# A two-layer decoder trunk on one core: one more hidden pair of the second feed-forward layer computed plainly, its operand combinations on VectorE alone, and other closing products among the last sums

## The chip, the core and the metric

The kernel runs on one core of a Trainium2 chip. The metric is the device time of one execution in microseconds; of several runs the median is given. TensorE does the matrix products, VectorE, ScalarE and GpSimd the elementwise work, SyncE issues the transfers. Each engine works through its own instructions in the order in which the program was built, and waits where a result of another engine is missing.

## The reference

A sequence of 1024 tokens of width 1024, with 16 meta tokens ahead, runs through two layers. Layer 0 mixes tokens by causal pooling, layer 1 by differential attention with 8 heads; after each mixer comes a SwiGLU feed-forward part with 2816 hidden units. All is float32.

```
def rms_norm(x, g):
    y = xf * lax.rsqrt(jnp.mean(xf * xf, axis=-1, keepdims=True) + RMS_EPS)
    return y * g
def swiglu(h, w_gate, w_up, w_down):
    return (jax.nn.silu(h @ w_gate) * (h @ w_up)) @ w_down
...
    for i in range(DEPTH):
        hn = rms_norm(h, mix_norm_g[i])
        if i % N_MIXERS == 0:
            h = h + pool_mixer(hn, pool_w[j], pool_scale[j])
        else:
            h = h + diff_attention(hn, attn_w_qkv[j], attn_w_o[j], ...)
        h = h + swiglu(rms_norm(h, ffn_norm_g[i]), ffn_w_gate[i], ffn_w_up[i], ffn_w_down[i])
    h = rms_norm(h, final_norm_g)
    return h[:, N_META:]
```

## The kernel before

**Precision.** A float32 product is made of three matmuls on rounded numbers (`mm3`, lines 167 to 172): each operand is kept as a rounded high half and a low half, the rest, and high x high, high x low and low x high are added up in PSUM. Whatever goes into a product must therefore be split first: ScalarE rounds it (a CAST), and VectorE or GpSimd subtracts the rounded half from it (`split`, line 1304, for the second feed-forward part; `split_w`, line 147, elsewhere).

**Tiles.** Activations lie with the features on the 128 partitions and tokens along the row. The feed-forward part of layer 1 (`layer1`, from line 1556) works in two halves of 512 tokens, `x[0]` and `x[1]` (x10 and x11 in the program's names), each of eight feature blocks. The 2816 hidden units are 22 slices of 128, taken as 11 pairs. For each pair, gate and up products come first, then silu(gate) x up (`acts1`, or the `use` functions), then the pair's share of the down product (`yd`), which VectorE adds to the residual `H` (`down_add`, line 1496).

**Two ways to a gate or up product.** `plain_up` (line 1381) multiplies a slice by a half of the tokens: 16 products of three matmuls for gate and up together. `wino` (line 1392) handles a pair of slices and both token halves as a 2 x 2 block product with seven block multiplications instead of eight (Strassen and Winograd). It needs combinations of weight blocks (`z`, on GpSimd, line 1420) and of token blocks. The latter, T1 to T4, serve all pairs and are made once by the generator `twist_gen` (line 1323): for each of four feature blocks k, t3 = b22 - b12, t1 = b12 - b11, t2 = b22 - t1, each from the high and low halves and split again. The differences of the high halves (`d`) run on VectorE, those of the low halves (`e`) on GpSimd, and the low half of the split on GpSimd. T4 overwrites a part of x[1] and is undone before the last pair, which is plain as well.

**The order.** Pair 0 is plain, pairs 1 to 9 use `wino`. The generator is advanced by hand between the steps of pair 0 (`next(tw)`, with `fill` of the down product). The final place of each instruction on its engine is decided by a scheduler that builds the program from a simulated timeline; only the very end is written out (`manual_schedule`).

**The attention entry.** Ahead of layer 1 the last sums of layer 0 run beside the first norm of layer 1 (`rstd_gen`, line 174: ScalarE squares each feature block, `sq`, and GpSimd adds them into `acc`; TensorE sums over partitions, `ms`, and spreads the result, `mr`). Beside it the first heads' weights are loaded and split: `proj_w` (line 880) takes head 0's three on VectorE and later heads' on GpSimd, in four pieces.

**The end.** The last pair's down product is made for tokens 0 to 511 (chunk 1), 512 to 767 (chunk 2) and 768 to 1023 (chunk 0). `final` (line 1530) closes each chunk with the final norm: eight closing products H x gain x r, six on VectorE in one instruction each (line 1550), two, of chunk 0 three, on GpSimd (line 1548) after ScalarE has applied the gain (line 1547).

Of the kernel before, what the change touches and what calls it, by code (L numbers as in the profile page):

```python
# [11 lines left out]
ALU = mybir.AluOpType  # L12
# [87 lines left out]
class Trunk:  # L100
# [73 lines left out]
    def rstd_gen(self, out, h, a, b, nm, lag=9, wide=False, ys=None):  # L174
# [1148 lines left out]
    def twist_gen(self, x):  # L1323
# [13 lines left out]
        def less(nm, a, b):  # L1337
            d = self.tt(f"{nm}d")
            V.tensor_tensor(d, a[0], b, op=ALU.subtract)
            V.tensor_tensor(d, d, a[1], op=ALU.add)  # L1340
            return d
# [13 lines left out]
        for k in range(4):  # L1355
            b11, b12, b21, b22 = ([part(j, i, hl, k) for hl in range(2)] for i in range(2) for j in range(2))
            t3 = diff(f"t3_{k}", b22, b12)
            self.split(t3, *pair(3, k), G)
            t1 = diff(f"t1_{k}", b12, b11)
            self.split(t1, *pair(1, k), G)  # L1360
            t2 = less(f"t2_{k}", b22, t1)
            self.split(t2, *pair(2, k), G)
            yield
        yield True
        for k in range(4):
            t4 = diff(f"t4_{k}", [part(0, 1, hl, k) for hl in range(2)], [t.bitcast(F32) for t in pair(2, k)])
            self.split(t4, *pair(4, k), G if k % 2 else V)
            yield
        yield True
        for k in range(4):  # L1370
            b12 = diff(f"b12_{k}", [part(0, 0, hl, k) for hl in range(2)], [t.bitcast(F32) for t in pair(1, k)], ALU.add)
# [158 lines left out]
    def final(self, c, ys=None):  # L1530
        nc, ap = self.nc, self.ap
        w, o = W1[c], OFF1[c]
        h = self.H[:, :, o : o + w]
        ro = {}
        for n, _ in enumerate(self.rstd_gen(ro, h, 0, w, f"fin{c}", FINLAG[c], c == 1, ys)):
# [3 lines left out]
            yield  # L1539
        r = ro[f"fin{c}"]  # L1540
        yield
        pk = (1, 4, 6) if ys else (1, 4)
        for k in range(KT):
            hk = h[:, k, :]
            if k in pk:
                if not ys:
                    nc.scalar.activation(hk, hk, AF.Copy, scale=self.gcol("fin", k))
# [3 lines left out]
            yield  # L1551
            if k in OUTS[c]:
                k0 = OUTS[c][k]
                nc.sync.dma_start(ap["out"].rearrange("(k p) n -> p k n", p=P)[:, k0 : k + 1, o : o + w], h[:, k0 : k + 1, :])

    def layer1(self, ox, ws, part):
        nc, tc, ap = self.nc, self.tc, self.ap
        NP = FT // 2
        with ExitStack() as right, ExitStack() as left:
# [30 lines left out]
            def plain(j, s):  # L1590
                if s not in gu:
                    gu[s] = self.gu_units(s, f"c{s}{j}")
                yield from self.plain_up(s, x, j * HALF, HALF, gu[s], s, a)
# [6 lines left out]
            drain(plain(1, 1))  # L1600
            next(tw)
            drain(plain(1, 0))
            next(tw)
            dg = self.down_gen(0, a)
            while not next(tw):
                fill(dg, 2)
            while not next(tw):
                fill(dg, 1)
            drain(dg)
            for p in range(1, NP - 1):  # L1610
                s = {}
                drain(self.gate_gen(p, x, s))
                if p > 1:
                    drain(self.down_gen(p - 1, a))
# [214 lines left out]
```

## Time and profile before

| | us |
|---|---|
| median of 3 runs | 2135.73 |
| lowest and highest run | 2135.21, 2138.09 |
| the profiled execution | 2137.84 |
| its span, first to last instruction | 2136.1 |
| TensorE busy in it | 2073.9 (97%) |
| VectorE busy | 1359.7 (64%) |
| ScalarE busy | 883.6 (41%) |
| GpSimd busy | 589.0 (28%) |

The span is what the profiler sees of the profiled execution; that execution's own time has 1.7 us more around it, and is 2.1 us above the median. PE is TensorE, DVE VectorE, ACT ScalarE, POOL GpSimd. In a row, L with a number is the line of the kernel, `out<-in` are tile names without their numbers, then come partitions x elements; brackets give the idle time of the engine ahead of the instruction and who ended it. The granted clock of TensorE is a share of its full 2.4 GHz. Consecutive instructions of one engine overlap a little, so that durations add up to more than the time from one start to the next.

### The profile page before, as it was taken

What the parts mean: (1) busy time and instruction counts of PE and PEld (TensorE: products, weight loads), DVE (VectorE), ACT (ScalarE), POOL (GpSimd) and SP (SyncE); (2) the same over time, 40 slices, a digit from 0 to 9 for tenths busy, and PEclk for the clock granted to TensorE, in tenths of its full rate; (3) what the DMA queues carried; (4) which work ended last, traced back from release to release, by engine and by line L of the source; (5) the groups of instructions that cost most, each with busy time, mean ns of one, the idle gap of its engine ahead of it and who ended that gap; (6) DMA issues with size and microseconds to landing.
All of it is one profiled execution on the core that took longest, in us unless ns stands there. A gap on an engine that the chain in (4) does not pass through costs nothing.

```text
span 2136.1 us, 30678 instructions
## 1 busy us (share of the span) xinstructions
PE 2073.9 (97%) x11958; PEld 1923.6 (90%) x11958; DVE 1359.7 (64%) x2363; ACT 883.6 (41%) x1860; POOL 589.0 (28%) x692
## 2 busy tenths in 40 slices
PE   7999999999999999999999999998999999999996
PEld 7999999999999999999999998876788888888886
DVE  6665555555555467776676777479666666666655
ACT  5533222333232235666666655342433333333223
POOL 4301111101111026443444333137312112222103
PEclk8999999999999999999999999998999999999998
DMA  7002111111110132121111146411111111111102
GB/s 251 22 22 70 40 50 50 50 60 40 40 60 20 50 116 89 43 63 42 60 63 43 53 134 207 153 41 40 60 40 60 60 59 40 60 60 40 60 21 79
DMA packets 52700, 139.30 MB, mean 65 GB/s; under 512 B 5618, under 2 KB 17435, under 8 KB 52555
## 3 DMA queue, kind: packets, MB, share of 16 engines
q1 hardware_dynamic: 52555, 137.34, 19.3%
q8 instruction: 94, 1.54, 0.3%
q14 instruction: 51, 0.42, 0.1%
HBM read 115.16 MB, written 17.90 MB: 62 GB/s over the span
## 4 chain that ended last, share of the span: by engine, by line
PE 86%; DVE 7%; ACT 3%; DMA 2%; issue 1%; POOL 0%; SPq 0%; DVEq 0%; ACTq 0%; POOLq 0%
PE pj L170 4%; PE pj L171 4%; PE pj L172 4%; PE y L170 3%; PE y L172 3%; PE y L171 3%; PE yd L170 3%; PE yd L171 3%; PE yd L172 3%; PE xw_g L172 3%; PE xw_g L170 3%; PE xw_g L171 3%; PE gu L171 3%; PE xw_u L172 3%; PE xw_u L170 3%; PE xw_u L171 3%
## 5 line engine op out<-in xcount | busy, mean ns | idle before, releaser
L170 PE MATMUL pj<-xh_m,w_h 128*128 128x348 f32 (+2 forms) x576 | 187.5, 326 | 1.3 <-DVE oo L1091 1.1
L172 PE MATMUL pj<-xh_m,w_l 128*128 128x348 f32 (+2 forms) x576 | 184.8, 321 | 0.0
L171 PE MATMUL pj<-xl_m,w_h 128*128 128x348 f32 (+2 forms) x576 | 184.3, 321 | 0.0
L1496 DVE TENSOR_TENSOR H<-H,yd 128x512 f32<-128x512 f32 (+1 forms) x184 | 120.4, 662 | 88.7 <-PE yd L172 87.5
L820 DVE TENSOR_TENSOR h<-h,y 128x348 f32<-128x348 f32 (+1 forms) x216 | 108.4, 514 | 81.7 <-PE y L172 81.6
L170 PE MATMUL yd<-ah,d 128*128 128x512 f32 (+1 forms) x368 | 141.8, 390 | 12.0 <-DVE H L1496 7.2
L1305 ACT CAST w_u<-raw_u 128x512 fp32r<-128x512 f32 x91 | 55.0, 621 | 228.5 <-PE y L172 115.3
L171 PE MATMUL yd<-al,d 128*128 128x512 f32 (+1 forms) x368 | 141.9, 386 | 0.5 <-DVE al L1306 0.5
L172 PE MATMUL yd<-ah,d 128*128 128x512 f32 (+1 forms) x368 | 140.5, 385 | 0.0
L170 PE MATMUL y<-ah,d 128*128 128x348 f32 (+1 forms) x432 | 138.3, 320 | 0.0
L171 PE MATMUL y<-al,d 128*128 128x348 f32 (+1 forms) x432 | 138.0, 320 | 0.0
L172 PE MATMUL y<-ah,d 128*128 128x348 f32 (+1 forms) x432 | 135.7, 320 | 0.0
L1306 DVE TENSOR_TENSOR w_g<-raw_g,w_g 128x512 fp32r<-128x512 f32 x91 | 76.1, 842 | 66.9 <-ACT w_g L1305 60.3
L170 PEld LDWEIGHTS pj<-xh_m,w_h 128*128 128x128 f32 x576 | 108.4, 188 | 2.2 <-DVE oo L1091 1.3
L171 PEld LDWEIGHTS pj<-xl_m,w_h 128*128 128x128 f32 x576 | 108.5, 189 | 0.7
L172 PEld LDWEIGHTS pj<-xh_m,w_l 128*128 128x128 f32 x576 | 108.3, 188 | 0.3
L1011 ACT ACTIVATE e<-s,st 128x144 f32<-128x144 f32 (+6 forms) x112 | 78.8, 705 | 39.6 <-DVE e L1021 20.0
L170 PEld LDWEIGHTS yd<-ah,d 128*128 128x128 f32 x368 | 70.6, 193 | 26.7 <-DVE H L1496 8.2
L1420 POOL TENSOR_TENSOR z<-raw_g 128x512 f32<-128x512 f32 x18 | 27.2, 1514 | 241.8 <-DVE w_u L1306 241.8
L1306 DVE TENSOR_TENSOR d<-raw_d,d 128x512 fp32r<-128x512 f32 x80 | 68.1, 863 | 39.0 <-ACT d L1305 38.9
L1305 ACT CAST w_g<-raw_g 128x512 fp32r<-128x512 f32 x91 | 56.5, 623 | 79.6 <-PE xw_u L172 35.0
L1043 DVE TENSOR_TENSOR atl<-at,ath 116x512 fp32r<-116x512 f32 (+3 forms) x112 | 62.0, 571 | 39.5 <-ACT ath L1042 39.1
(597 smaller groups left out, 6542.2 us busy)
## 6 DMA issues: line engine op xcount, KB each, us to landing
raw_d<-in_down_dram SPq DMA_DIRECT2D x42, 512.0 KB, 4.0
raw_g<-in_gate_dram SPq DMA_DIRECT2D x38, 512.0 KB, 3.5
raw_u<-in_up_dram SPq DMA_DIRECT2D x38, 512.0 KB, 3.9
raw_w<-in_wqkv_dram SPq DMA_DIRECT2D x24, 512.0 KB, 3.3
odram<-oo SPq DMA_DIRECT2D x28, 256.0 KB, 2.0
ox<-odram SPq DMA_DIRECT2D x4, 1536.0 KB, 9.3
qk<-qk SPq DMA_DIRECT2D x16, 260.0 KB, 2.9
raw_woe<-in_wo_dram SPq DMA_DIRECT2D x8, 512.0 KB, 3.3
```

The source lines that it names most:

```text
L170: nc.tensor.matmul(out, wh, xh, start=first, stop=False, skip_group_check=skip)
L171: nc.tensor.matmul(out, wh, xl, start=False, stop=False, skip_group_check=skip)
L172: nc.tensor.matmul(out, wl, xh, start=False, stop=last, skip_group_check=skip)
L820: nc.vector.tensor_tensor(h, h, ps, op=ALU.add)
L1011: nc.scalar.activation(ev, main[m], AF.Exp, bias=nm, accum_out=sm)
L1043: nc.vector.tensor_tensor(al[:rows, b0 : b0 + len(grp), :], pt[:rows, : len(grp), :], hv.bitcast(F32), op=ALU.subtract)
L1305: self.nc.scalar.copy(hi, src)
L1306: (eng or self.nc.vector).tensor_tensor(lo, src, hi.bitcast(F32), op=ALU.subtract)
L1420: G.tensor_tensor(S[o], a, b, op=op)
L1496: self.nc.vector.tensor_tensor(h, h, ps, op=ALU.add)
```

## The change

Three places of the built order change.

1. Pair 1 of layer 1's feed-forward part becomes plain, too. Its slice 2 is worked on first and last, so its weights are loaded and split twice. The combinations are spread over the plain products and pair 0's down product by a helper that advances the generator every few steps (`paced`). They are computed as t3 = b22 - b12, t2 = b11 + t3, t1 = b12 - b11, all on VectorE with their splits; only the final undoing of T4 stays partly on GpSimd.
2. At the end, `final` is divided into the statistic (`final_rstd`) and the closing products (`final_out`). The eight of chunk 1 are distributed: four in a row, four among the sums of chunk 0's down product; chunk 2's eight stand among and behind the later ones. For these two chunks none is left on GpSimd, and ScalarE's multiplication by the gain goes.
3. Head 0's third weight (`wi == 2`) has its low half made on GpSimd.

```diff
-    def rstd_gen(self, out, h, a, b, nm, lag=9, wide=False, ys=None):
+    def rstd_gen(self, out, h, a, b, nm, lag=9, wide=False, ys=None, extra=None):
...
             if ys:
                 next(ys)
+                next(extra)
...
+        if ys:
+            drain(extra)
         yield from self.rstd_tail(out, terms, w, nm, wide)
...
-            s["w"][wi] = self.load_w(self.ap["wqkv"][wi * NH + h], self.wp, f"w{wi}_{h}", "w", self.nc.gpsimd if h else None, 4)
+            s["w"][wi] = self.load_w(self.ap["wqkv"][wi * NH + h], self.wp, f"w{wi}_{h}", "w", self.nc.gpsimd if h or wi == 2 else None, 4)
...
-        def diff(nm, a, b, op=ALU.subtract):
+        def diff(nm, a, b, op=ALU.subtract, eng=V):
             d, e = self.tt(f"{nm}d"), self.tt(f"{nm}e")
             V.tensor_tensor(d, a[0], b[0], op=op)
-            G.tensor_tensor(e, a[1], b[1], op=op)
+            eng.tensor_tensor(e, a[1], b[1], op=op)
             V.tensor_tensor(d, d, e, op=ALU.add)
...
             t3 = diff(f"t3_{k}", b22, b12)
-            self.split(t3, *pair(3, k), G)
+            self.split(t3, *pair(3, k))
+            yield
+            t2 = more(f"t2_{k}", b11, t3)
+            self.split(t2, *pair(2, k))
+            yield
             t1 = diff(f"t1_{k}", b12, b11)
-            self.split(t1, *pair(1, k), G)
-            t2 = less(f"t2_{k}", b22, t1)
-            self.split(t2, *pair(2, k), G)
+            self.split(t1, *pair(1, k))
             yield
...
-            self.split(t4, *pair(4, k), G if k % 2 else V)
+            self.split(t4, *pair(4, k))
...
+            def paced(gen, side, step):
+                for n, _ in enumerate(gen):
+                    if n % step == step - 1 and side:
+                        if next(side[0], True):
+                            side.clear()
...
-            drain(plain(1, 1))
-            next(tw)
-            drain(plain(1, 0))
-            next(tw)
-            dg = self.down_gen(0, a)
-            while not next(tw):
-                fill(dg, 2)
-            while not next(tw):
-                fill(dg, 1)
-            drain(dg)
-            for p in range(1, NP - 1):
+            paced(seq(plain(1, 1), plain(1, 0)), [tw], 4)
+            paced(self.down_gen(0, a), [tw], 2)
+            a = self.new_a(1)
+            one = [tw]
+            paced(seq(plain(1, 2), plain(1, 3)), one, 4)
+            while one and not next(tw):
+                pass
+            del gu[2]
+            paced(seq(plain(0, 3), plain(0, 2)), [tw], 3)
+            for p in range(2, NP - 1):
...
-            drain(seq(aa(1, 2), self.down_chunk(p, us, a, OFF1[2], W1[2])), self.final(1))
-            drain(aa(1, 0), self.final(2))
+            drain(seq(aa(1, 2), self.down_chunk(p, us, a, OFF1[2], W1[2])), self.final_rstd(1, ro))
+            o1 = self.final_out(1, ro)
+            tail = self.final_rstd(2, ro)
+            for n, _ in enumerate(aa(1, 0)):
+                next(tail, None)
+                if n % 2:
+                    next(o1)
+            drain(tail)
+            extra = seq(o1, self.final_out(2, ro))
             with tc.manual_schedule(engines=ORD):
-                drain(self.final(0, self.down_last(p, us, a, OFF1[0], W1[0])))
+                drain(self.final_rstd(0, ro, self.down_last(p, us, a, OFF1[0], W1[0]), extra))
+                drain(self.final_out(0, ro, (1, 4, 6)))
```

**GpSimd at the attention entry, before.** acc_m_7428 is the sum of squares of the first token chunk, acc_m_7702 of the second; w_1_l is the low half of the next head's first weight.

```order
L199 TENSOR_TENSOR acc_m_7428<-acc_m_7428,sq_m_4_7440 128x348
L199 TENSOR_TENSOR acc_m_7428<-acc_m_7428,sq_m_5_7443 128x348
L199 TENSOR_TENSOR acc_m_7428<-acc_m_7428,sq_m_6_7446 128x348
L199 TENSOR_TENSOR acc_m_7428<-acc_m_7428,sq_m_7_7449 128x348
L160 TENSOR_TENSOR w_1_l<-raw_w_1_8235,w_1_h 128x256 x4
L199 TENSOR_TENSOR acc_m_7702<-sq_m_0_7703,sq_m_1_7705 128x348
L199 TENSOR_TENSOR acc_m_7702<-acc_m_7702,sq_m_2_7708 128x348
```

**The same, changed.** Here w_0_l is the low half of head 0's third weight.

```order
L200 TENSOR_TENSOR acc_m_7428<-acc_m_7428,sq_m_4_7440 128x348
L160 TENSOR_TENSOR w_0_l<-raw_w_0_7685,w_0_h 128x256 x4
L200 TENSOR_TENSOR acc_m_7428<-acc_m_7428,sq_m_5_7443 128x348
L160 TENSOR_TENSOR w_1_l<-raw_w_1_8235,w_1_h 128x256 x4
L200 TENSOR_TENSOR acc_m_7428<-acc_m_7428,sq_m_6_7446 128x348
L200 TENSOR_TENSOR acc_m_7702<-sq_m_0_7703,sq_m_1_7705 128x348
L200 TENSOR_TENSOR acc_m_7428<-acc_m_7428,sq_m_7_7449 128x348
```

The eight pieces of the two weights stand among the last additions of the first chunk, the last of which is now behind all of them.

**VectorE at the start of layer 1's feed-forward part, before.** The rows lead to s1_0_512, the product of slice 0 and the second token half, whose rounded half the down product yd_0 needs; x11 and x10 are the token halves, d_0_ a down weight, w1_g_1 a weight of pair 1.

```order
L1306 TENSOR_TENSOR d_0_2_15368<-raw_d_0_15269,d_0_2_15368 128x512
L1332 TENSOR_TENSOR t3_1d_15231<-x_f11_0_15011 128x512
L1332 TENSOR_TENSOR t1_1d_15238<-x_f11_0_15011,x_f10_0_14802 128x512
L1306 TENSOR_TENSOR d_0_3_15417<-raw_d_0_15269,d_0_3_15417 128x512
L1378 TENSOR_TENSOR s1_0_512_15226<-gu1_0_512_15177,s1_0_512_15226 128x512
L1496 TENSOR_TENSOR H_14565<-H_14565,yd_0_0_0_15275 128x512
L1306 TENSOR_TENSOR w1_g_1_15465<-raw_g_1_15459,w1_g_1_15465 128x512
L1334 TENSOR_TENSOR t3_1d_15231<-t3_1d_15231,t3_1e_15232 128x512
L1306 TENSOR_TENSOR al_0_14866<-s1_0_512_15226,ah_0_14865 128x512
```

**The same place, changed.**

```order
L1383 TENSOR_TENSOR s1_0_512_15233<-gu1_0_512_15170,s1_0_512_15233 128x512
L1343 TENSOR_TENSOR t2_1d_15276<-t2_1d_15276,x_f10_1_14803 128x512
L1336 TENSOR_TENSOR t3_2e_15359<-x_f11_2_15013,x_f11_1_15012 128x512
L1309 TENSOR_TENSOR c21_00_15410<-raw_c21_15407,c21_00_15410 128x512
L1501 TENSOR_TENSOR H_14565<-H_14565,yd_0_0_0_15244 128x512
L1337 TENSOR_TENSOR t1_1d_15316<-t1_1d_15316,t1_1e_15317 128x512
L1309 TENSOR_TENSOR al_0_14866<-s1_0_512_15233,ah_0_14865 128x512
L1337 TENSOR_TENSOR t3_2d_15358<-t3_2d_15358,t3_2e_15359 128x512
L1309 TENSOR_TENSOR T21_15111<-t2_1d_15276,T20_15110 128x512
L1501 TENSOR_TENSOR H_14565<-H_14565,yd_0_1_0_15260 128x512
L1309 TENSOR_TENSOR T11_15113<-t1_1d_15316,T10_15112 128x512
L1501 TENSOR_TENSOR H_14565<-H_14565,yd_0_2_0_15284 128x512
```

The product has the high and the low halves' combinations (names with d and e) around it, and T rows, the combinations' low halves, have come to VectorE. Five rows later in the same queue, after t2_2d, t1_2d, t1_2e, t3_3d and one T row, stands the sum of yd_0_0_512.

**VectorE at the end, before.** Chunk 1's six closing products stand together ahead of sums of chunk 2, and chunk 2's six, in the second excerpt, ahead of those of chunk 0.

```order
L1550 SCALAR_TENSOR_TENSOR H_14565<-H_14565,vec_75,acc_fin1_19563 128x512 x6
L1496 TENSOR_TENSOR H_14565<-H_14565,yd_10_4_512_19666 128x256
L1496 TENSOR_TENSOR H_14565<-H_14565,yd_10_5_512_19674 128x256
L1496 TENSOR_TENSOR H_14565<-H_14565,yd_10_6_512_19682 128x256
L1496 TENSOR_TENSOR H_14565<-H_14565,yd_10_7_512_19701 128x256
```

```order
L1550 SCALAR_TENSOR_TENSOR H_14565<-H_14565,vec_75,acc_fin2_19736 128x256 x6
L1496 TENSOR_TENSOR H_14565<-H_14565,yd_10_0_768_19838 128x256
L1496 TENSOR_TENSOR H_14565<-H_14565,yd_10_1_768_19839 128x256
L1496 TENSOR_TENSOR H_14565<-H_14565,yd_10_2_768_19840 128x256
L1496 TENSOR_TENSOR H_14565<-H_14565,yd_10_3_768_19841 128x256
```

**The end, changed,** where chunk 0's sums begin.

```order
L1501 TENSOR_TENSOR H_14565<-H_14565,yd_10_0_768_19807 128x256
L1555 SCALAR_TENSOR_TENSOR H_14565<-H_14565,vec_75,acc_fin1_19554 128x512
L1501 TENSOR_TENSOR H_14565<-H_14565,yd_10_1_768_19808 128x256
L1555 SCALAR_TENSOR_TENSOR H_14565<-H_14565,vec_75,acc_fin1_19554 128x512
L1501 TENSOR_TENSOR H_14565<-H_14565,yd_10_2_768_19809 128x256
L1555 SCALAR_TENSOR_TENSOR H_14565<-H_14565,vec_75,acc_fin1_19554 128x512
L1501 TENSOR_TENSOR H_14565<-H_14565,yd_10_3_768_19810 128x256
L1555 SCALAR_TENSOR_TENSOR H_14565<-H_14565,vec_75,acc_fin1_19554 128x512
```

Between the two of them only four of chunk 1's products are left in a row; the other four alternate with these sums, and chunk 2's follow in the same way.

## Rows read from the trace of the kernel before

**Rows 1.** The page: busy time by engine, and the chain that ended last.
```profile
PE 2073.9 (97%) x11958; PEld 1923.6 (90%) x11958; DVE 1359.7 (64%) x2363; ACT 883.6 (41%) x1860; POOL 589.0 (28%) x692
...
PE 86%; DVE 7%; ACT 3%; DMA 2%; issue 1%; POOL 0%; SPq 0%; DVEq 0%; ACTq 0%; POOLq 0%
```

**Rows 2.** Windows (start:end, length, then busy time and instruction count by engine, granted clock).
```profile
1440.00:1516.00 76.00, 61.68 (x234) 48.39 (x233) 71.14 (x72) 22.32 (x38) 52.35 (x34) 0.87 0.12 42
1560.00:1636.00 76.00, 76.00 (x337) 62.94 (x336) 47.71 (x65) 23.01 (x40) 14.14 (x9) 1.00 0.14 53
```

**Rows 3.** What TensorE waited for, 1395 to 1540 us.
```profile
PE yd L170 <- DVE H L1496: 5.4, 2, 4.7
PE yd L170 <- ACT ah L1305: 4.3, 1, 4.3
PE y_g L172 <- DVE w_g L1306: 3.7, 1, 3.7
```

**Rows 4.** Timeline of TensorE (start, duration, operation, idle time before).
```profile
1483.02 0.79 PE L170 MATMUL yd<-ah,d 128*128 128x512 f32 x1 [4.73 <-DVE H L1496]
1484.04 0.63 PE L172 MATMUL yd<-ah,d 128*128 128x512 f32 x1
1484.47 0.63 PE L170 MATMUL yd<-ah,d 128*128 128x512 f32 x1
```

**Rows 5.** Windows at the attention entry and in the feed-forward part.
```profile
799.25:802.00 2.75, 2.75 (x11) 2.75 (x11) 1.90 (x4) 1.74 (x5) 0.83 (x1) 0.50 0.35 125
1484.00:1488.00 4.00, 4.00 (x11) 3.09 (x10) 4.00 (x7) 1.24 (x2) 3.23 (x2) 0.50 0.00 0
```

**Rows 6.** Timeline of VectorE, 1431 to 1462 us.
```profile
1431.55 0.74 DVE L1297 SCALAR_TENSOR_TENSOR xt_f<-H,vec,r_f 128x512 f32<-128x512 f32 x1
...
1441.41 0.68 DVE L1332 TENSOR_TENSOR t_0d<-x_f 128x512 f32<-128x512 f32 x1
...
1459.38 1.74 DVE L1306 TENSOR_TENSOR d<-raw_d,d 128x512 fp32r<-128x512 f32 x1
1461.05 0.68 DVE L1378 TENSOR_TENSOR s<-gu,s 128x512 f32<-128x512 f32 x1
1461.65 0.67 DVE L1496 TENSOR_TENSOR H<-H,yd 128x512 f32<-128x512 f32 x1
```

**Rows 7.** Timeline of GpSimd, then of ScalarE, same stretch.
```profile
1460.54 1.73 POOL L1333 TENSOR_TENSOR t_1e<-x_f,x_f 128x512 f32<-128x512 f32 x1
...
1456.20 0.60 ACT L1377 ACTIVATE s<-gu 128x512 f32<-128x512 f32 x1
```

**Rows 8.** Timeline of GpSimd, ScalarE, TensorE at the attention entry.
```profile
786.34 3.13 POOL L199 TENSOR_TENSOR acc_m<-acc_m,sq_m 128x348 f32<-128x348 f32 x3
...
794.16 3.04 POOL L160 TENSOR_TENSOR w_l<-raw_w,w_h 128x256 fp32r<-128x256 f32 x4 [0.23 <-ACT w_h L156]
...
793.04 1.05 ACT L156 CAST w_h<-raw_w 128x1024 fp32r<-128x1024 f32 x1 [1.00 <-DMA raw_w<-in_wqkv_dram]
...
796.43 1.28 ACT L240 ACT_TABLE_LOAD   x1
...
795.71 0.67 PE L217 MATMUL ms_m<-ones,acc_m 128*116 128x1 f32 x6
...
798.25 1.32 PE L245 MATMUL mr_m<-ident,st_m 116*128 116x116 f32 x6 [1.87 <-DVE st_m L241]
```

**Rows 9.** Timeline of VectorE, then of TensorE, at the end.
```profile
2098.87 6.63 DVE L1550 SCALAR_TENSOR_TENSOR H<-H,vec,acc_fin 128x512 f32<-128x512 f32 x6 [1.39 <-ACT acc_fin L246]
...
2105.42 1.40 DVE L1496 TENSOR_TENSOR H<-H,yd 128x256 f32<-128x256 f32 x4
...
2126.06 0.17 DVE L239 TENSOR_REDUCE st_fin<-ms_fin 116x2 f32<-116x6 f32 x1 [1.78 <-PE ms_fin L217]
...
2110.83 1.10 PE L217 MATMUL ms_fin<-ones,acc_fin 128*116 128x1 f32 x6 [5.46 <-POOL acc_fin L199]
...
2116.69 0.39 PE L170 MATMUL yd<-ah,d 128*128 128x256 f32 x1 [0.52 <-ACT acc_fin L246]
```

More of the change, by code (lines that the diff above doesn't have):

```diff
@@ L1328, in part, with more @@
             return self.part8(x[j], hl, 4 * i + k).bitcast(F32)
-        def diff(nm, a, b, op=ALU.subtract):
+        def diff(nm, a, b, op=ALU.subtract, eng=V):
             d, e = self.tt(f"{nm}d"), self.tt(f"{nm}e")
             V.tensor_tensor(d, a[0], b[0], op=op)
-            G.tensor_tensor(e, a[1], b[1], op=op)
+            eng.tensor_tensor(e, a[1], b[1], op=op)
             V.tensor_tensor(d, d, e, op=ALU.add)
             return d
-        def less(nm, a, b):
+        def more(nm, a, b):
             d = self.tt(f"{nm}d")
-            V.tensor_tensor(d, a[0], b, op=ALU.subtract)
+            V.tensor_tensor(d, a[0], b, op=ALU.add)
             V.tensor_tensor(d, d, a[1], op=ALU.add)
@@ L1370, in twist_gen @@
         for k in range(4):
-            b12 = diff(f"b12_{k}", [part(0, 0, hl, k) for hl in range(2)], [t.bitcast(F32) for t in pair(1, k)], ALU.add)
+            b12 = diff(f"b12_{k}", [part(0, 0, hl, k) for hl in range(2)], [t.bitcast(F32) for t in pair(1, k)], ALU.add, G)
             self.split(b12, *pair(4, k), G)
@@ L1528, in down_last, with final_rstd @@
             yield
-    def final(self, c, ys=None):
-        nc, ap = self.nc, self.ap
+    def final_rstd(self, c, ro, ys=None, extra=None):
+        nc = self.nc
         w, o = W1[c], OFF1[c]
         h = self.H[:, :, o : o + w]
-        ro = {}
-        for n, _ in enumerate(self.rstd_gen(ro, h, 0, w, f"fin{c}", FINLAG[c], c == 1, ys)):
+        for _ in self.rstd_gen(ro, h, 0, w, f"fin{c}", FINLAG[c], c == 1, ys, extra):
             if ys:
@@ L1539, in final, with final_out @@
             yield
+    def final_out(self, c, ro, pk=()):
+        nc, ap = self.nc, self.ap
+        w, o = W1[c], OFF1[c]
+        h = self.H[:, :, o : o + w]
         r = ro[f"fin{c}"]
-        yield
-        pk = (1, 4, 6) if ys else (1, 4)
         for k in range(KT):
@@ L1545, in final @@
             if k in pk:
-                if not ys:
-                    nc.scalar.activation(hk, hk, AF.Copy, scale=self.gcol("fin", k))
                 nc.gpsimd.tensor_tensor(hk, hk, r[:, :w], op=ALU.mult)
@@ L1554, in final @@
                 nc.sync.dma_start(ap["out"].rearrange("(k p) n -> p k n", p=P)[:, k0 : k + 1, o : o + w], h[:, k0 : k + 1, :])
+            yield
     def layer1(self, ox, ws, part):
@@ L1588, in layer1, with plain @@
             gu = {}
[L1590 to L1593, printed above, removed]
+            def plain(j, f):
+                if f not in gu:
+                    gu[f] = self.gu_units(f, f"c{f}{j}")
+                yield from self.plain_up(f, x, j * HALF, HALF, gu[f], f % 2, a)
+            def paced(gen, side, step):
[3 more added lines that the diff above has]
+                            side.clear()
             drain(seq(plain(0, 0), plain(0, 1)), n1)
@@ L1599, in layer1 @@
             tw = self.twist_gen(x)
[L1600 to L1610 removed]
+            paced(seq(plain(1, 1), plain(1, 0)), [tw], 4)
[8 more added lines that the diff above has]
+            for p in range(2, NP - 1):
                 s = {}
                 drain(self.gate_gen(p, x, s))
[L1613 to L1614 removed]
+                drain(self.down_gen(p - 1, a))
                 a = self.new_a(p)
@@ L1635, in layer1 @@
             drain(self.down_chunk(p, us, a, OFF1[1], W1[1]))
-            drain(seq(aa(1, 2), self.down_chunk(p, us, a, OFF1[2], W1[2])), self.final(1))
-            drain(aa(1, 0), self.final(2))
+            ro = {}
+            drain(seq(aa(1, 2), self.down_chunk(p, us, a, OFF1[2], W1[2])), self.final_rstd(1, ro))
[7 more added lines that the diff above has]
+            extra = seq(o1, self.final_out(2, ro))
             with tc.manual_schedule(engines=ORD):
-                drain(self.final(0, self.down_last(p, us, a, OFF1[0], W1[0])))
+                drain(self.final_rstd(0, ro, self.down_last(p, us, a, OFF1[0], W1[0]), extra))
+                drain(self.final_out(0, ro, (1, 4, 6)))
     def run(self):
```

1 line of the change is left out of this document (removed).

## The prediction

> **What bounds the kernel now.** I read the page's busy times first, then the chain of waits, then what TensorE waits for, then the windows and timelines of the three places that the change moves. TensorE is busy for 2073.9 of 2136.1 us and holds 86% of the chain that ended last [rows 1]. So a microsecond counts where TensorE stands still or runs slowly, and VectorE's work counts where TensorE waits for it.
>
> The largest such place is the start of the second layer's feed-forward part. Two windows of 76 us show it [rows 2]: between 1440 and 1516 us TensorE ran 234 matmuls, in the undisturbed stretch from 1560 it ran 337 of the same kind. The missing 103 cost 103 x 76/337 = **23.2 us**. In the disturbed window VectorE is busy for 71.1 of 76 us and GpSimd for 52.4, later for 47.7 and 14.1. TensorE's waits there are three of about 4 us each, with smaller ones, and all are for results that came late from VectorE: a rounded half that ScalarE could make only after VectorE's product (4.3), the sums into H (5.4 in two), the low half of a weight (3.7) [rows 3]. They make some 13 of the 23 us. The rest is clock: after the wait of 4.73 us that ended at 1483.02 the matmuls start every 0.43 us [rows 4], against 76/337 = 0.2255 in the quiet stretch, and in the 4 us from 1484 the granted clock is 0.50 [rows 5], the lower of the two levels, 1.2 instead of 2.4 GHz.
>
> Why is VectorE late? Its 128x512 operation with both operands in SBUF takes 0.68 us at 1441.41 and 1.74 at 1459.38, with the next start 1.67 later [rows 6]; at that time GpSimd is at work on SBUF operands as well, 1.73 us for one [rows 7]. The sum into H at 1461.65, with one operand in PSUM, takes 0.67 with GpSimd still running, and starts 0.60 after the instruction ahead of it [rows 6]. So the slow pace belongs to both engines at once on SBUF operands, and without GpSimd I price every 128x512 operation of VectorE at 0.60 from start to start.
>
> **The change, part by part.**
>
> *Stalls removed, -23.2.* GpSimd has no combination left in this stage. By its built order VectorE issues 111 instructions from the first combination to the last, beside 384 matmuls: 67 us at 0.60, against 87 at 0.2255. VectorE has 20 us to spare over the stage, so I let all three waits go. The 0.60 may not hold; that is the third rival.
>
> *Second pair plain, +5.4.* Its gate and up products are 192 matmuls where seven-for-eight needed 168: 24 x 0.2255 = 5.4 us, all on TensorE. The reloaded slice (a third load of a gate and an up slice, 12 weight splits instead of 8) costs nothing while VectorE has its 20 us, which cover its four further splits; without them each is 0.6 us.
>
> *What is late next, +2.7.* The second order excerpt shows it: 16 instructions stand between s1_0_512 and the sum of yd_0_0_512. The product can start some 0.9 us after its slice's last matmul, 0.60 for ScalarE's function [rows 7] and an estimated 0.3 for handing over, so the sum ends 0.9 + 18 x 0.60 = 11.7 us after it. By the built order TensorE wants the rounded half 8 matmuls on, at 1.8, and gets it at 0.9 + 0.6 + some 0.7 = 2.2; it wants the sum's PSUM buffer 45 matmuls on, at 10.2 + 0.4. Waits: 0.4 and 1.1 us. After a wait of 1.87 us at the attention entry [rows 8] the clock was 0.50 for 2.75 us, in which 11 small matmuls ran [rows 5]: half of that, here taken as 1.2, is lost. Together 2.7. Ends: 0.5, if the queue is ahead; 9, if a wait of the old size with its clock remains.
>
> *Attention entry, +4.1.* Head 0's third weight is split on GpSimd now. The first order excerpt shows its four pieces ahead of sq_5 and the next head's four ahead of sq_6. GpSimd ends sq_4 at 789.47; four pieces take 3.04; sq_5 ends at 793.5; the next head's rounding, which waited for a load, ends at 794.09, its pieces at 797.1; three additions of about 1.0 end at 800.1 [rows 8]. TensorE wants that sum at 795.71 and can't pass it. From the statistic to the next matmul on it some 1.25 us remain, for 1.28 of the present 2.54 is a table load that will be over by then [rows 8]: 801.35 instead of 798.25, +3.1. The wait of 4.4 us is followed by the lower clock for longer, with 2.2 us lost as in [rows 4] (11 matmuls at 0.43) instead of 1.2: +1.0. TensorE bounds what follows, so nothing hides this. VectorE gains its four pieces there, for which no one waits. Ends: +1, if the pieces find gaps that I don't see, and +7, if the load comes later.
>
> *The end, -2.4.* Six closing products of 128x512 stand in a row ahead of sums, 6.63 us, beside two on GpSimd [rows 9]. Four are left there, alone: 0.66 each by the row at 1431.55 less the overlap of 0.08 [rows 6], so 2.6, and what follows comes 4.0 earlier. TensorE's statistic at 2110.83, which waited 5.46 us for GpSimd [rows 9], comes some 3.6 earlier, and so does the restart of the down product, 2113.1 instead of 2116.69 [rows 9]. From there VectorE bounds: its first sum at about 2114.4, and up to its last addition eight sums (0.34 each, from the four in 1.40 [rows 9]), four products of 128x512 (0.66), four of 128x256 (some 0.40) and two small additions (0.34): 7.6 us, 2122.0. Before, that addition ended at 2124.28, 1.78 us ahead of the reduction at 2126.06 [rows 9]. That is 2.3 earlier, and the four products that are left, 1.6 us, nearly fit into the 1.78: I take -2.4 with the overlaps. The rest is unchanged. Ends: -4 if the chain ahead decides, +1 if the products delay the sums more.
>
> *The sum.* -23.2 + 5.4 + 2.7 + 4.1 - 2.4 = -13.4 us. The profiled execution took 2137.84, so it would take 2124.4. It lies 2.1 above the median of the runs shown, 2135.73, which becomes **2122.3 us**.
>
> **The rivals.**
> *VectorE stays late.* In the window from 1440 it is busy for 71.1 of 76 us, and it takes on GpSimd's combinations, some 24 instructions: with no gain in pace, 24 x 0.60 = 14 more make 85.5 of the 87 us of matmuls, no slack, and one stall of the old size, 23.2/3 = 7.7 us, stays in place of my 2.7: 2127.3. Two make 2135.0, no change. The Trainium skill ("Perfetto Trace Analysis", Optimizing Scalar/DVE Operations) advises the opposite move, to offload a saturated VectorE, though between it and GpSimd that might not help. For this rival: sums stand behind runs of five combinations. Against: the 0.68 beside the 1.74 [rows 6].
> *The entry absorbs its detour.* If the pieces cost TensorE nothing, 4.1 fewer: 2118.2. Against it: GpSimd works in order, and the statistic needs its last addition.
> *Slower: the long duration belongs to the operands, not to GpSimd.* If two SBUF operands of this stage cost 1.67 us on their own, the 89 such instructions among the 111 take 149 us and the rest 13, 162 against 87 on TensorE. The stage, 104.8 us now (87 - 5.4 + 23.2), grows by 57, and with the entry and the end the kernel takes about 2194. It decides from 1.0 us an instruction on: (103 - 13)/89. Against it stands the same kind of row at 0.68 with GpSimd idle [rows 6].
> *It does less than it says.* TensorE's order at the end is as it was; if its waits don't move either, 2.4 more: 2124.7.
>
> **How the numbers follow.** The forecast, with 2118 to 2126 around it and the last rival inside, has 0.62; the absorbed entry 0.13; one old stall 0.14; two old stalls 0.06; slower 0.05 (the operands, or three old stalls, 2142.7). A measurement of this kernel can tell about 0.2%, 4.3 us, from no change. Faster is 0.62 + 0.13 + 0.14 = 0.89, the same 0.06, slower 0.05. The terms' bounds give 2115.4 (all low) to 2134.9 (all high); I keep 2115.5 to 2131, which leaves out the two-stall and slower cases and a little below.
>
> **What would show it.** Right: VectorE's two-operand rows near 0.68 from 1440 on; no combination on GpSimd; the waits of 4 us gone, one of 1 to 2 for H in the first down product; 24 more matmuls; a wait of some 4 us for GpSimd's sum at 796, with the lower clock after it; the statistic near the end waiting 2 us rather than 5.5. Wrong: VectorE rows above 1 us without GpSimd beside them, a stall over 3 us for H or for a weight's low half, or no new wait at the attention entry.

## The result, and the profile after

Four runs of the change have a median of 2125.73 us (2123.49 to 2126.71), four of the kernel before, in the same comparison, 2136.39 (2135.21 to 2138.09). The ratio is 0.9948, 95% interval 0.9931 to 0.9965: 10.7 us faster, at 2125.7 where 2122.3 was forecast, inside the range. The profiled execution took 2126.26 us with a span of 2124.5, so its span is 11.6 shorter than before. Medians and ratios, here and below, leave disturbed runs out.

Where they went is read from the start of the same matmul in both traces: the offset (after less before), and how it changes over a stretch of before's time.

| stretch of before, us | what lies there | change of offset | forecast |
|---|---|---|---|
| 0 to 780 | layer 0, all of it in the first 60 us | +2.2 | 0 |
| 780 to 850 | attention entry | +5.3 | +4.1 |
| 850 to 1427 | attention | +0.2 | 0 |
| 1427 to 1441 | norm ahead of the feed-forward part | -3.1 | 0 |
| 1441 to 1600 | feed-forward part, first pairs | -14.2 | -23.2 + 5.4 + 2.7 = -15.1 |
| 1600 to the last instruction | other pairs, the end | -2.1 | -2.4 |

The page, rows as in [rows 1]:

```profile
PE 2074.1 (98%) x11982; PEld 1927.2 (91%) x11982; DVE 1332.7 (63%) x2379; ACT 877.6 (41%) x1846; POOL 532.3 (25%) x658
...
PE 88%; DVE 5%; ACT 3%; DMA 2%; POOL 1%; issue 1%; SPq 0%; DVEq 0%; ACTq 0%; POOLq 0%
```

TensorE runs the 24 more matmuls and holds 88% of the chain instead of 86%. Windows of the change, the answer to [rows 2, 5]:

```profile
1440.00:1516.00 76.00, 74.21 (x320) 60.73 (x319) 64.51 (x101) 26.37 (x45) 10.71 (x6) 0.98 0.16 56
1464.00:1468.00 4.00, 3.89 (x10) 3.07 (x11) 4.00 (x8) 1.63 (x4) 0.00 (x0) 0.59 0.65 251
800.00:804.00 4.00, 1.32 (x6) 1.24 (x6) 0.00 (x0) 2.81 (x5) 3.92 (x5) 0.50 0.76 263
804.00:808.00 4.00, 3.64 (x14) 3.64 (x15) 1.61 (x4) 1.36 (x4) 1.21 (x2) 0.50 0.01 2
```

The stage ran 320 matmuls where [rows 2] had 234, and VectorE did 101 instructions in less busy time than it had needed for 72. What TensorE still waited for from 1395 to 1540 us, the answer to [rows 3]:

```profile
PE gu L171 <- DVE x_f L1304: 3.7, 2, 2.8
PE yd L170 <- ACT ah L1308: 1.8, 1, 1.8
```

The first is the norm of the second token half, the second is new. The timeline there, VectorE, then ScalarE, GpSimd and TensorE:

```profile
1444.00 1.78 DVE L1336 TENSOR_TENSOR t_0e<-x_f 128x512 f32<-128x512 f32 x1
...
1448.71 0.68 DVE L1309 TENSOR_TENSOR T<-t_0d,x_f 128x512 fp32r<-128x512 f32 x1
...
1462.12 0.68 DVE L1309 TENSOR_TENSOR d<-raw_d,d 128x512 fp32r<-128x512 f32 x1
1462.72 0.68 DVE L1383 TENSOR_TENSOR s<-gu,s 128x512 f32<-128x512 f32 x1
...
1460.42 0.60 ACT L1382 ACTIVATE s<-gu 128x512 f32<-128x512 f32 x1
...
1463.44 0.62 ACT L1308 CAST ah<-s 128x512 fp32r<-128x512 f32 x1 [1.91 <-DVE s L1383]
...
1443.60 1.63 POOL L1304 TENSOR_TENSOR x_f<-xt_f,x_f 128x512 fp32r<-128x512 f32 x1 [1.28 <-ACT x_f L1302]
...
1438.50 0.50 PE L171 MATMUL gu<-x_f,c 128*128 128x512 f32 x1 [2.81 <-DVE x_f L1304]
1438.84 0.40 PE L172 MATMUL gu<-x_f,c 128*128 128x512 f32 x1
...
1464.11 0.74 PE L170 MATMUL yd<-ah,d 128*128 128x512 f32 x2 [1.79 <-ACT ah L1308]
```

From the first combination, at 1442.79, to 1468 us VectorE's rows are at 0.68 or 0.69 with one exception, at 1444.00, beside the GpSimd row shown; the next long one, at 1509.61, stands beside GpSimd's work for pair 2. The silu of the second half ends at 1461.02; its product starts on VectorE only at 1462.72, because VectorE had had no gap since 1450.68, with the rows of the combinations ahead of it. The rounded half follows, and TensorE waits 1.79 us, with a granted clock of 0.59 in the 4 us behind it.

The attention entry, timelines of GpSimd, ScalarE and TensorE, the answer to [rows 8] (this trace stands 2.2 later from its first 60 us):

```profile
792.15 3.00 POOL L160 TENSOR_TENSOR w_l<-raw_w,w_h 128x256 fp32r<-128x256 f32 x4
...
797.03 2.77 POOL L160 TENSOR_TENSOR w_l<-raw_w,w_h 128x256 fp32r<-128x256 f32 x4 [0.98 <-PE y L172]
799.75 0.92 POOL L200 TENSOR_TENSOR acc_m<-acc_m,sq_m 128x348 f32<-128x348 f32 x1
...
801.58 0.88 ACT L189 ACTIVATE sq_m<-h 128x348 f32<-128x348 f32 x2 [0.39 <-POOL acc_m L200]
802.47 1.28 ACT L243 ACT_TABLE_LOAD   x1
...
802.48 1.32 PE L220 MATMUL ms_m<-ones,acc_m 128*116 128x1 f32 x6 [5.47 <-POOL acc_m L200]
804.36 1.63 PE L248 MATMUL mr_m<-ident,st_m 116*128 116x116 f32 x6 [0.56 <-DVE st_m L244]
```

TensorE waits 5.47 us for GpSimd's sum, and the lower clock, 0.50, stands in both windows behind. The table load was not over by then: ScalarE's last squares waited for GpSimd's additions, and the load stands behind them in ScalarE's order. It ends at 803.75, and TensorE's six matmuls of the sum, 1.32 us at the lower clock, at 803.80: either alone would hold the statistic until then.

The end, timelines of VectorE and TensorE, the answer to [rows 9]:

```profile
2089.13 3.40 DVE L1555 SCALAR_TENSOR_TENSOR H<-H,vec,acc_fin 128x512 f32<-128x512 f32 x4 [1.15 <-ACT acc_fin L249]
...
2104.27 0.42 DVE L1501 TENSOR_TENSOR H<-H,yd 128x256 f32<-128x256 f32 x1 [5.24 <-PE yd L172]
...
2111.96 0.41 DVE L200 TENSOR_TENSOR acc_fin<-acc_fin,sq_fin 128x256 f32<-128x256 f32 x1
...
2096.73 0.70 PE L220 MATMUL ms_fin<-ones,acc_fin 128*116 128x1 f32 x6 [0.88 <-POOL acc_fin L200]
...
2112.42 0.70 PE L220 MATMUL ms_fin<-ones,acc_fin 128*116 128x1 f32 x6 [2.43 <-DVE acc_fin L200]
```

Four products stand in a row instead of six, the statistic waits 0.88 instead of 5.46 us, and the last wait has passed from GpSimd to VectorE.

### The profile page after: what moved, and what is told of

It is laid out like the page before. It is cut to its first block, busy times and chain, and to the rows that moved or that the text cites. A ratio compares the mean times of both kernels' runs of the same rounds, so it can differ in the third digit from the quotient of the medians.

```text
span 2124.5 us, 30680 instructions
## 1 busy us (share of the span) xinstructions
PE 2074.1 (98%) x11982; PEld 1927.2 (91%) x11982; DVE 1332.7 (63%) x2379; ACT 877.6 (41%) x1846; POOL 532.3 (25%) x658
## 4 chain that ended last, share of the span: by engine, by line
PE 88%; DVE 5%; ACT 3%; DMA 2%; POOL 1%; issue 1%; SPq 0%; DVEq 0%; ACTq 0%; POOLq 0%
PE pj L172 4%; PE pj L170 4%; PE pj L171 4%; PE yd L170 4%; PE yd L172 4%; PE yd L171 4%; PE y L170 4%; PE y L171 3%; PE y L172 3%; PE gu L171 3%; PE gu L172 3%; PE gu L170 3%; PE xw_g L172 3%; PE xw_g L170 3%; PE xw_g L171 3%; PE xw_u L170 3%
```

## The experiments

The edits are against the change unless the text says otherwise. The stage is the start of layer 1's feed-forward part. The theory: the stage was slow because GpSimd's combinations slowed VectorE's, and the entry pays for the weight that GpSimd took over. Its rivals: the plain pair does the work, or the spreading, or the two-operand rows are slow by themselves. The last two columns are changes of offset against before in single traces, worked out as in the table above. The stretch from 1441 us repeats well: the change, e3 and e6 have -14.2 there, each.

| run | median, us | ratio to before, 95% | entry, 780 to 850 | 1427 to 1600 (of it before 1441) |
|---|---|---|---|---|
| the change | 2125.73 | 0.9948 (0.9931 to 0.9965) | +5.3 | -17.2 (-3.1) |
| e1 weight back | 2120.2 | 0.9923 (0.9908 to 0.9937) | -0.4 | -17.3 (-1.1) |
| e2 weight alone | 2143.31 | 1.0030 (1.0018 to 1.0042) | +4.7 | -3.0 (-3.0) |
| e4 plain, with GpSimd | 2128.18 | 0.9962 (0.9948 to 0.9975) | +4.8 | -11.8 (-3.0) |
| e7 VectorE, not plain | 2133.65 | 0.9983 (0.9974 to 0.9992) | -0.2 | -3.3 (-1.1) |
| e11 e7 and z on VectorE | 2134.7 | 0.9980 (0.9970 to 0.9989) | -0.5 | -5.8 (-1.1) |
| e9 not spread | 2139.69 | 1.0005 (0.9996 to 1.0014) | +4.6 | -3.2 (-3.0) |
| e10 not spread, T4 late | 2123.64 | 0.9933 (0.9907 to 0.9959) | +4.5 | -18.8 (-3.1) |
| e5 reads on GpSimd | 2135.8 | 0.9992 (0.9983 to 1.0002) | +5.0 | -4.8 (-0.2) |
| e6 writes on GpSimd | 2124.18 | 0.9930 (0.9908 to 0.9953) | +5.0 | -17.2 (-3.0) |
| e3 old end | 2127.00 | 0.9953 (0.9941 to 0.9966) | +4.5 | -17.3 (-3.0) |
| e8 e1, sparser | 2119.73 | 0.9910 (0.9895 to 0.9926) | -1.5 | -17.7 (-1.1) |
| e12 e10, weight back | 2122.49 | 0.9922 (0.9909 to 0.9934) | 0.0 | -16.9 (-1.1) |

**The attention entry: e1 and e2.** e1 gives the weight back to VectorE in the change; e2 makes only this edit, in the kernel before, with the opposite sign.

```diff
-    ..., self.nc.gpsimd if h or wi == 2 else None, 4)
+    ..., self.nc.gpsimd if h else None, 4)
```

> The change with one part undone: head 0's third weight is split on VectorE again. If GpSimd's queue at the attention entry is what costs there (5.3 us between the two traces, from 780 to 850 us), the wait of 5.5 us for GpSimd's sum goes and the kernel takes some 5 us less than the change, about 2120.5. Rival: the entry is late because of what runs ahead of it (the opening of the changed kernel's trace is 2.1 us longer), and the split is hidden: within 1.5 us of the change, 2124 to 2127. A last possibility, that VectorE needed the relief: slower than the change.

> The kernel before with that one part alone: head 0's third weight split on GpSimd. If the entry's cost is its own, about 5 us slower than before, 2141; a wait of 4 to 6 us for GpSimd's sum of squares at about 800 us shows in the trace. Rival, hidden: within 1.5 us of before.

TensorE at the entry, first in e1, then in e2:

```profile
799.41 0.74 PE L220 MATMUL ms_m<-ones,acc_m 128*116 128x1 f32 x6 [0.84 <-DVE h L577]
802.54 0.92 PE L248 MATMUL mr_m<-ident,st_m 116*128 116x116 f32 x6 [2.39 <-DVE st_m L244]
```

```profile
802.75 1.32 PE L217 MATMUL ms_m<-ones,acc_m 128*116 128x1 f32 x6 [5.48 <-POOL acc_m L199]
```

The wait for GpSimd goes and comes with this one edit, and with it 5 us of the entry. In all eight profiles with the weight on GpSimd the entry takes 4.5 to 5.3 us more than in before's, in the five without it 0.0 to 1.5 less. By the medians the weight costs the kernel 5.5 us in the change (2125.73 less 2120.2) and 5.9 alone (2143.31 less 2137.44, before's median beside it). A small credit comes with it: in all eight profiles with the weight on GpSimd the wait for the norm of the second half, before 1441, is 2.81 to 2.83 us long, in the six others 3.16 or 3.17, and in seven of the eight the clock stays at 1.00 behind it. The credit is some 2 us: -3.0 before 1441 in those seven, -1.1 already in the five others, whose clock recovers sooner than in before's profile. Why that wait is shorter wasn't tried. In the change the credit buys nothing: TensorE comes 2 us earlier to the rounded half that is late, so that e1, without the credit, gains the same 17 us up to 1600. In e2's trace entry and norm leave 4.7 - 3.0 = 1.7 us, and 3.0 more lie in the first 60 us; the 5.9 of the medians is more than the two stretches explain, and the rest stays open.

**Which part gains in the feed-forward part: e4, e7, e11.** e4 keeps the plain pair, with its spreading and the late T4, and gives the low differences and low halves back to GpSimd:

```diff
-        def diff(nm, a, b, op=ALU.subtract, eng=V):
+        def diff(nm, a, b, op=ALU.subtract, eng=G):
...
-            self.split(t3, *pair(3, k))
+            self.split(t3, *pair(3, k), G)
```

(and so for t2, t1 and odd blocks of T4). e7 is the kernel before with the reverse: no plain pair, the combinations on VectorE. e11 is e7 with the weight combinations z of pair 1 on VectorE, too.

```diff
-            G.tensor_tensor(e, a[1], b[1], op=op)
+            eng.tensor_tensor(e, a[1], b[1], op=op)
...
-            G.tensor_tensor(S[o], a, b, op=op)
+            (V if p == 1 else G).tensor_tensor(S[o], a, b, op=op)
```

(eng is VectorE but for the undoing of T4; the second pair of lines is e11's alone.)

> The change with the combinations' low differences and low halves on GpSimd again, everything else as in the change (second pair plain, spread over it). If the two engines slow each other on operands in SBUF, VectorE's rows go back to 1.7 us wherever GpSimd runs beside it, though the instructions have a longer stage to fit in: some 5 to 12 us slower than the change, 2131 to 2138. Rival: the plain pair and the spreading are what removed the waits, and the engine matters little: within 2 us of the change; VectorE has fewer instructions then, so it could even be faster.

> The kernel before with the combinations on VectorE alone, and nothing else: the second pair in seven products, combinations as early as before, no change at the end or at the attention entry. If GpSimd's company was the cost, most of the 23 us of stalls go without the 24 additional matmuls: 8 to 18 us faster than before, 2118 to 2128. Rival: VectorE is just too full for this stage, and needs the plain pair for time: no more than 4 us faster than before, or slower, with waits of several us for low halves of T and for H.

> The run with the combinations on VectorE alone and the second pair in seven products, with that pair's eight combinations of weight blocks on VectorE too, so that GpSimd does nothing between the second half's norm and the third pair. In the run without this step, four of them ran beside VectorE from 1449.7 to 1456.4 and four of VectorE's rows took 1.78 us there, 4.4 us in all, ahead of a wait of 3.0 us. If GpSimd's company is all that keeps this order slow, 4 to 8 us less than that run, ratio to the kernel before 0.9945 to 0.9965. Rival: VectorE is too full for this stage without the plain pair's time; eight more instructions there take 4.8 us, and the ratio stays at 0.9975 to 1.0.

Windows of e4, of e7 and of e11 (columns as in [rows 2]):

```profile
1440.00:1516.00 76.00, 69.42 (x296) 55.92 (x295) 62.78 (x69) 22.34 (x38) 43.25 (x28) 0.96 0.16 56
```

```profile
1440.00:1516.00 76.00, 62.44 (x251) 48.37 (x249) 66.58 (x97) 23.65 (x40) 17.65 (x9) 0.93 0.13 42
```

```profile
1440.00:1516.00 76.00, 64.99 (x262) 51.06 (x261) 65.14 (x107) 25.00 (x42) 2.06 (x2) 0.93 0.12 42
```

e11 has GpSimd idle, and VectorE gets through 107 instructions in 65 us, as in the change, yet TensorE runs 262 matmuls instead of 320. So VectorE's pace alone does not free TensorE. e7's waits for VectorE's results:

```profile
PE xw_g L170 <- ACT w_g L1305: 3.1, 1, 3.1
PE yd L170 <- ACT ah L1305: 3.0, 1, 3.0
PE xw_u L172 <- DVE w_u L1306: 2.6, 1, 2.6
```

Two of them are for pair 1's own weights, which a pair of seven products wants behind the combinations. e4, with GpSimd still busy for 43 us (52 before) and VectorE slowed (69 instructions in 63 us), runs 296: the plain pair leaves out that demand for 192 matmuls. Taken from 1441, where the norm's clock no longer counts: plain alone -8.7, VectorE alone -2.2 (with z -4.7), both -14.2. The rival that the plain pair does most of it stands; it keeps a wait of 5.87 us for a rounded half, of which the change has 1.79 left:

```profile
1466.58 1.22 PE L170 MATMUL yd<-ah,d 128*128 128x512 f32 x2 [5.87 <-ACT ah L1308]
```

e7 and e11 came out as their rivals expected, e4 between its theory and its rival. By the ratios e4 and the change differ by 0.0014, 3.0 us, and e7 and e11 by 0.0003, 0.6 us, within their intervals. So the 5.5 us that GpSimd's company costs beside the plain pair (14.2 less 8.7), and the 2.5 that z brings without it (4.7 less 2.2), are shown by the traces of this stage alone.

**Spreading: e9 and e10.** Both let the generator run as densely as before, three steps (one feature block) behind each plain block, then three for two steps of the down product. In e9 T4 is made within the down product, in e10 behind pair 1's plain products; the last lines of this cut are e10's.

```diff
-            paced(seq(plain(1, 1), plain(1, 0)), [tw], 4)
-            paced(self.down_gen(0, a), [tw], 2)
+            drain(plain(1, 1))
+            for _ in range(3):
+                next(tw)
...
-            paced(seq(plain(1, 2), plain(1, 3)), one, 4)
-            while one and not next(tw):
+            drain(seq(plain(1, 2), plain(1, 3)))
+            while not next(tw):
```

In e9, not in e10, pair 1's products with the second token half read blocks that T4 has already overwritten.

> The change with its combinations not spread: they stand as densely as before, two blocks' between the plain products of pair 0 and the rest in its down product, all on VectorE; the second pair is plain. If the plain pair is what counts because VectorE's results are then needed 192 matmuls later, the time stays within 3 us of the change, 2123 to 2129. Rival: spreading is what counts, since sums into H would wait behind the dense block as before: two waits of 2 to 5 us with the lower clock after them, 6 to 12 us more than the change, 2132 to 2138.

> As the run without spreading, but the combination that overwrites a block of the second token half is left for after the products of pair 1 that read this half, as in the change; the other three combinations stand as densely as before, all on VectorE, with the second pair plain. The run without spreading lost 14 us at one wait of 8.3 us for that overwritten block and had no more waits than the change ahead of it. If this block's place is all that the spreading is worth, the time is that of the change within 3 us: ratio to the kernel before 0.993 to 0.9965. Rival: spreading matters for the sums into H too, 4 us or more above the change, ratio 0.9967 or more.

TensorE in e9:

```profile
1495.58 1.22 PE L170 MATMUL gu<-x_f,c 128*128 128x512 f32 x2 [8.29 <-ACT x_f L1308]
1498.55 0.80 PE L171 MATMUL gu<-x_f,c 128*128 128x512 f32 x1 [1.74 <-DVE x_f L1309]
```

All that e9 loses is this wait, for T4, and its lower clock: up to 1476 us it ran 145 matmuls from 1440, the change 143. With T4 behind the plain products (e10) the wait is gone, and the time is that of the change within its interval. The spreading is worth nothing that can be measured; the place of T4 is worth 16 us by the two medians. So e9 took a little more than the time that its rival expected, but for another reason.

**Two engines on SBUF: e5 and e6.** 24 operations are added to GpSimd among the combinations, for no result that is used. In e5 each reads two 128x512 tiles, in e6 one column of them, and then writes a whole tile.

```diff
+        def more_work(hi, lo):
+            for i in range(2):
+                G.tensor_tensor(self.z[i], hi.bitcast(F32), lo.bitcast(F32), op=ALU.add)
```

```diff
+                G.tensor_tensor(self.z[i][:, :1], hi[:, :1].bitcast(F32), lo[:, :1].bitcast(F32), op=ALU.add)
+                G.memset(self.z[i], 0.0)
```

> The change with 24 additional GpSimd additions of 128x512, each reading one combination's two halves when they are ready and writing a tile that nothing uses. VectorE's instructions and their order stay the same but for two. If a GpSimd instruction on SBUF operands beside it is what makes VectorE's two-operand instruction take 1.7 instead of 0.68 us, such rows are back and VectorE loses up to 24 x 1.07 = 26 us in the stage, of which its idle time hides most: 3 to 12 us more than the change. Rival: the long rows belong to what the combinations read; no change, within 2 us, and rows of 0.68.

> As the run with 24 additional GpSimd additions, but each of the 24 reads only one column and then fills its tile of 128x512 with zeros. If it is GpSimd's reading of whole SBUF operands that makes VectorE's instruction long, VectorE's rows stay at 0.68 and the time is that of the change within 2 us. Rival: any 128x512 work of GpSimd does it, then rows of over 1 us are back and the time is 3 us or more above the change.

VectorE, then GpSimd in e5:

```profile
1451.02 1.78 DVE L1335 TENSOR_TENSOR t_0d<-x_f,x_f 128x512 f32<-128x512 f32 x1
1452.73 1.78 DVE L1309 TENSOR_TENSOR c<-raw_c,c 128x512 fp32r<-128x512 f32 x1
...
1452.21 3.45 POOL L1360 TENSOR_TENSOR z<-T,T 128x512 f32<-128x512 f32 x2
```

The same in e6:

```profile
1449.10 0.68 DVE L1309 TENSOR_TENSOR c<-raw_c,c 128x512 fp32r<-128x512 f32 x1
1449.71 0.68 DVE L1336 TENSOR_TENSOR t_0e<-x_f,x_f 128x512 f32<-128x512 f32 x1
...
1449.77 0.99 POOL L1361 MEMSET z<- 128x512 f32 x2
```

The same instruction of VectorE takes 1.78 us beside GpSimd's reads and 0.68 beside its writes. GpSimd was busy for 40 of the 76 us in e5 and 32 in e6; 1427 to 1600 grew by 12.4 us against the change in the one, 2.8 of them at the norm (last section), and by nothing in the other. The medians agree: 10.1 us above the change and 1.6 below it, within the interval. The Trainium skill ("SBUF — State Buffer", Who interferes with whom) says that a VectorE instruction with two SBUF inputs contends with a GpSimd instruction that reads SBUF, not with one that only writes it; these rows agree on both.

**The end: e3.** The change with `final` as before at the end.

```diff
-            o1 = self.final_out(1, ro)
-            tail = self.final_rstd(2, ro)
...
+            drain(seq(aa(1, 2), self.down_chunk(p, us, a, OFF1[2], W1[2])), self.final(1))
+            drain(aa(1, 0), self.final(2))
```

> The change with the end as before: six closing products of the first 512 tokens in a row on VectorE and two on GpSimd, the same for the next 256. If the moved products are worth what the two traces show (2.1 us to the end of the span, 4.9 at the statistic in between), the kernel takes about 2 us more than the change, 2128, and the wait of 5.5 us for GpSimd's last addition is back. Rival: a tail that gains in the middle loses it before the end, so 0 to 1 us.

What TensorE waits for in e3, 2050 us to the end:

```profile
PE ms_fin L217 <- POOL acc_fin L199: 6.2, 2, 5.5
```

The wait of 5.5 us is back. In the two traces the end is 2.6 us longer than in the change from 2080 us on; the medians, of different comparisons, differ by 1.3, within their intervals. All the traces show the sign: from 1600 us to the last instruction the nine with the new end take 1.8 to 3.9 us less than before, the four with the old one 0.7 less to 0.5 more.

**A better version: e8 and e12.** e8 is e1 with fewer combinations ahead of the second half's product; e12 is e10 with the weight back.

```diff
-            paced(seq(plain(1, 1), plain(1, 0)), [tw], 4)
+            paced(seq(plain(1, 1), plain(1, 0)), [tw], 6)
```

> The change with the weight's split back on VectorE and fewer combinations ahead of the last product of pair 0's slice 0 (one step of them in six products instead of four). VectorE is busy without a gap from the norm of the second token half to that product in the change. If this queue sets the wait of 1.8 us there and the lower clock after it, both go, and the kernel takes 1 to 4 us less than with the weight's split alone put back: ratio to the kernel before 0.9905 to 0.9918. Rival: the combinations are late at the next sums instead, same ratio, 0.9923 or above.

> The two undone parts that gained, together: combinations t1 to t3 dense as before, T4 late, second pair plain, and the weight's split at the attention entry back on VectorE. If the gains add (5 us for the weight, 1.5 to 3 for the dense order), about 2117.5, ratio 0.9895 to 0.9915, like the run with sparser combinations. Rival: they overlap, ratio 0.992 or more.

VectorE in e8:

```profile
1456.40 0.69 DVE L1383 TENSOR_TENSOR s<-gu,s 128x512 f32<-128x512 f32 x1
```

The product no longer stands in a queue; TensorE waits for no rounded half, and only 0.5 us for a sum. e8 has the lowest median, 2119.73, ratio 0.991: ahead of both kernels, though not measurably of e1. e12 did not add e1's gain to e10's: the entry's 4.5 us went, but 1.9 of the next stage came back, the norm's clock above all, and the medians differ by 1.2, as its rival expected.

## Why the prediction was right, and where it was not

**The size.** The three places are the ones forecast: +5.3, -14.2 and -2.1 make -11.0 where +4.1, -15.1 and -2.4 made -13.4. Two stretches that no term covered, +2.2 in the first 60 us and -3.1 at the norm, nearly cancel. By the medians it is 10.7.

**"Stalls removed, -23.2": the sum right, the reason half right.** All three waits went, as said, and the stage from 1441 agrees with the term: -23.2, 5.4 of more matmuls and 3.5 of a new wait (below) make -14.3 against -14.2. The mechanism is shown by e5 and e6, which also end the rival of the slow operands: 0.68 without GpSimd's reads. But the step gave the whole 23.2 to GpSimd's leaving ("GpSimd has no combination left in this stage"). The 87 us of matmuls that it set against VectorE's 67 already held the plain pair, which the next step booked as a cost of 5.4 and nothing else. Without that pair, VectorE alone gains 2.2 us (e7), 4.7 with z (e11); the pair with GpSimd's company 8.7 (e4), of 14.2 for both. So the size of the term rests on the pair as well, for which the step had counted no gain; in this the sum was lucky. What counted was not the work against the time of the whole stage, but what TensorE wants next: 192 matmuls that need no combination give VectorE the time to have them ready.

**"Second pair plain, +5.4"**: 24 more matmuls, as the page has it. The reloaded slice's splits made no wait of their own.

**"What is late next, +2.7": the size near, the place wrong.** The wait was 1.8 us, and 10 matmuls in the next 4 us instead of 4 / 0.2255 = 17.7 are 1.7 more: 3.5. It was for the rounded half, forecast at 0.4, not for the sum's PSUM buffer, forecast at 1.1. The step let VectorE take the product as soon as ScalarE's function was ready, and began its queue only there; VectorE was 1.7 us behind already, from combinations placed ahead of it. e8, which takes some of these away, has the product in time. The same rows dismiss the rival in which VectorE stays late by a whole old stall.

**"Attention entry, +4.1"**: shown by e1 and e2, 1.2 short. TensorE got its sum when forecast (802.48 less 2.7, its offset just ahead, is 799.8; forecast 800.1), but the step let the table load be over by then and priced the rest of the statistic at 1.25 us; it took 1.88. The load runs in ScalarE's order behind squares whose buffers GpSimd's detour holds. In the change the sum's matmuls at the lower clock end beside it, so this trace doesn't part the two; e6's does, where the sum ran faster and the function on it (`st_m`) still waited for the load:

```profile
801.42 1.28 ACT L243 ACT_TABLE_LOAD   x1
801.43 0.77 PE L220 MATMUL ms_m<-ones,acc_m 128*116 128x1 f32 x6 [3.86 <-POOL acc_m L200]
802.72 0.26 ACT L243 ACTIVATE st_m<-ms_m,eps 116x3 f32<-116x3 f32 x1
```

The lower clock behind it lasted through both windows. The rival "the entry absorbs its detour" is out.

**"The end, -2.4"**: -2.1. The statistic came 4.6 us earlier instead of 3.6 (2110.83 less 2096.73, less the offset of 9.5 ahead); two closing products no longer run on GpSimd ahead of its additions, which the step left out, and the rest was not taken apart; VectorE's stretch from the first sum to the last addition took 8.1 us (2104.27 to 2112.37) instead of 7.6.

**Not foreseen**: that the entry's edit reaches as far as the norm at 1431 us, where the wait became 0.35 us shorter and the clock stayed up.

## What to carry to other kernels

A helper engine's work is not weighed against the length of a stage but against the work that can go on without it up to each due time: here 24 more matmuls on the busiest engine bought 192 that need no helper, and that was worth more than a faster helper. Moving a second engine's reads away helps as far as the first engine then meets its due times (2.2 us here without the plain pair, 5.5 with it); ask, for each result that is wanted next, what stands ahead of it in the queue. And before work is given to an engine that is idle on average, look at what it does at that moment: four pieces ahead of a statistic's last addition cost 5 us, for a load of VectorE that nobody waited for.

## What the runs showed of the hardware that was not expected

**A wait of one length, two clocks.** The wait for the second half's norm was 2.81 us in the change (the row at 1438.50 above: the next matmul starts 0.34 later, clock 1.00), and 2.83 in e5, at the same place with the same matmuls ahead:

```profile
1437.33 0.80 PE L171 MATMUL gu<-x_f,c 128*128 128x512 f32 x1 [2.83 <-DVE x_f L1304]
1437.92 0.63 PE L172 MATMUL gu<-x_f,c 128*128 128x512 f32 x1
1438.35 0.63 PE L170 MATMUL gu<-x_f,c 128*128 128x512 f32 x1
```

There the clock is 0.50 over the 4 us behind it, which costs some 2.8 us (-0.2 before 1441 in the table instead of -3.0). It happened in one of eight profiles; the wait of 3.16 or 3.17 us was followed by 0.50 to 0.69 in all six that have it. In the change itself the shorter wait of 1.79 us was followed by 0.59.

**The opening varies.** The first 60 us, in which all kernels issue the same instructions, took between 0.1 us less and 4.6 us more than in the profile of before (e5, e1). The stretch from 850 to 1427 us, in which no edit lies either, took between 1.7 less (e7) and 1.7 more (e11). So the whole of a single trace carries 2 us and more, either way, that belong to no edit, and a change of a few us is better read by stretches. What sets these differences stays open.
